# Second halves of weight pairs split by ScalarE and an accumulating transfer in the last half of each MLP, and an eighth seven-product pair in the very last half

## Chip, cores and metric

One core of one Trainium2 chip runs the whole program. The metric is the device time of one launch in microseconds, as the median of several runs.

## What is computed

A two-layer trunk on x of 256 rows and 2048 columns in float32: layer 0 mixes tokens with a convolution module, layer 1 with latent attention, and each is followed by an MLP with squared ReLU. The change lies in the MLPs, in the product with `w2` (8192 x 2048):

```python
D_MODEL, SEQ, D_FF, DEPTH = 2048, 256, 8192, 2

def sq_relu_mlp(h, w1, w2):
    return jnp.square(jax.nn.relu(h @ w1)) @ w2

for layer in range(DEPTH):
    ...
    h = rms_norm(x, norm_mlp_g[layer])
    x = x + sq_relu_mlp(h, mlp_w1[layer], mlp_w2[layer])
return rms_norm(x, final_norm_g)
```

## The kernel before

Every float32 factor is split into a high part `hi` (rounded to the matmul's float32r type) and a low part `lo` = value minus `hi`. A product of two split factors is three matmuls (`mm3`, L203 to L205): high times high, low times high, high times low. ScalarE makes `hi` by a copy (L170, L497), VectorE makes `lo` by a subtraction (L174, L498). Weights come from HBM by SyncE's queue into `raw` (L160). Three `raw` buffers of 8 KB a partition and six buffers each of `hi` and `lo` of 4 KB (WB = 6) rotate, so the split of later weights runs ahead of TensorE by what these hold.

An MLP (`mlp`, called once for each layer) runs in two **halves** of the 8192 inner columns. A half first computes its 4096 inner columns (the up-projection, L655 and L656, from the turned input `xt` that lies at the right end of SBUF), eight groups of 512 columns; each group is squared, scaled and split again (L673 to L687). Then comes the down-projection with 4096 rows of `w2`, in two **passes** of 1024 output columns each (`Sums`, with all 8 PSUM banks). In a pass a unit of work is a **pair** of 128 rows by 1024 columns, for both blocks of 128 tokens:

- A *plain* pair takes 2 x 2 x 2 products of three matmuls, 24 in all. Its two rows are two weight pieces of 1024 columns; each is split by one ScalarE copy and one VectorE subtraction.
- A *mixed* pair takes seven products instead of eight (21 matmuls) in a Strassen-like scheme. VectorE pays for it: `mixed_weights` (L490 to L512) forms sums of weight blocks in place (L505, L506, L507) and splits seven blocks (three subtractions of 1024 columns and one of 512).

`MIXED` names the mixed pairs of each half: eight of sixteen (0, 1, 4, 5, 8, 9, 12, 13) in three halves, and seven, without 13, in the last half of layer 1. In a pass with eight, the order is plain, plain, mixed, mixed, plain, mixed, mixed, plain and so on; the last two are plain. Before the last pair `join` puts the mixed sums u1, u6, u7, u5 into `xs` (L586 to L591), and after it `close` adds the other four (L601, L604). In some passes the additions into `xs` are accumulating transfers from GpSimd's queue (`put`, L578).

The last pass of layer 1 (columns 1024 to 2047) runs through `product_A`: plain units of 4 x 128 rows by 512 columns for column block 2 (24 matmuls each), with mixed pairs (both column blocks) put between them by `between`, and then the plain units of column block 3. Before the change there are five units (the second has 2 x 128 rows and 12 matmuls), with 2, 1, 2 and 2 mixed pairs between them.

Each engine runs its instructions in the order in which the program lists them. That order was fixed when the program was built, and so were the places of the buffers.

```python
    def split_half(raw, h, eng):
        return lower_half(*upper_half(raw, h), eng)
    ...
        def plain(self, w, k, hi, lo, k0, end, middle=None):
            at_j = split(load([rows(w, k, 2, self.n * NB, 2 * NB)], 2), nc.vector)
    ...
            units = [list(range(4 * g, 4 * g + 4)) for g in plain]
            units[1:1] = [[2 * p, 2 * p + 1] for p in ps if p // 2 in mixed]
```

Of the kernel before, what the change touches and what calls it, by code (L numbers as in the profile page):

```python
# [38 lines left out]
PAD_RIGHT = 48  # L39
PAD_KV = 8  # L40
PAD_O = 56
WB = 6
# [37 lines left out]
def trunk_kernel(  # L80
# [83 lines left out]
    def upper_half(raw, h):  # L164

        _, nj, cols = raw.shape
        js = slice(h * nj // 2, (h + 1) * nj // 2)
        hi = wpool.tile([P, nj // 2, cols], F32R, tag="hi", name=nm("hi"), bufs=WB)
        lo = wpool.tile([P, nj // 2, cols], F32R, tag="lo", name=nm("lo"), bufs=WB)
        nc.scalar.activation(hi, raw[:, js, :], AF.Copy)  # L170
        return hi, lo, raw[:, js, :]

    def lower_half(hi, lo, raw, eng):
        eng.tensor_tensor(lo, raw, hi.bitcast(F32), op=ALU.subtract)  # L174
# [17 lines left out]
    def load_split(srcs, nj):  # L192
        return split(load(srcs, nj), nc.vector)
# [222 lines left out]

    def product_A(
        w, k_lo, nk, hi, lo, add, prepare, blocks=range(NNB), due=(), finish=None, before=None,
        units=None, banks=None, begun=None, beside=None, room=None,
    ):  # L420

        due = list(due)
# [9 lines left out]
        for n in blocks:  # L432
            ps = [acc_tile() for _ in range(T)] if banks is None else banks[n]

            n_end = 3 if finish is not None and n == blocks[-1] else 0
            wjs = []

            def products(u, t, to_end=True):
                for j, k in enumerate(units[u]):
                    mm3(  # L440
                        ps[t], hi(k, t), lo(k, t), *wjs[u](j),
                        first(ps[t]), u == nu - 1 - (not to_end) and k == units[u][-1],
                    )

            for u, ks in enumerate(units):
                if u == 0 and beside is not None:
                    beside(n, -1, due)
                wjs.append(load_split([rows(w, k_lo + ks[0], len(ks), n * NB, NB)], len(ks)))
                if u < nu - n_end:
                    for j, k in enumerate(ks):  # L450
                        for t in range(T):
                            mm3(ps[t], hi(k, t), lo(k, t), *wjs[u](j), first(ps[t]), u == nu - 1 and k == ks[-1])
                if banks is None:
                    while due:
                        prepare(due.pop(0))
                    step(-(-20 * 4 // nk) + 1 if nk > 4 * NNB else 6)
                elif n == blocks[-1]:
                    for _ in range(len(due) if n_end else min(1, len(due))):
                        prepare(due.pop(0), out=room)
                if beside is not None:  # L460
                    beside(n, u, due)
            if n_end:
                before()
                for t in range(T):


                    halves = t == T - 1
                    for u in range(nu - n_end, nu - halves):
                        products(u, t, not halves)
                    add(n, ps, t)  # L470
                    if not halves:
                        prepare(n, t)
                    else:
                        h = NB // 2
                        for c in range(2):
                            o = acc_tile()[:, :h]
                            for j, k in enumerate(units[-1]):
                                wh, wl = (w[:, c * h : (c + 1) * h] for w in wjs[-1](j))
                                mm3(o, hi(k, t), lo(k, t), wh, wl, j == 0, k == units[-1][-1])
                            add(n, {t: o}, t, c)  # L480
                            prepare(n, t, c)
                    finish(t)
            else:
                for t in range(T):
                    add(n, ps, t)
                due.append(n)
# [25 lines left out]
    def mixed_inputs(v, fh, fl):  # L512
# [15 lines left out]
        nc.vector.tensor_tensor(a12, a12, a11, op=ALU.subtract)  # L528
        halves(a, 3, 4)

    class Sums:


# [25 lines left out]
        def plain(self, w, k, hi, lo, k0, end, middle=None):  # L559

            at_j = split(load([rows(w, k, 2, self.n * NB, 2 * NB)], 2), nc.vector)
            order = [(j, c, t) for j in range(2) for c in range(2) for t in range(T)]
            if end:
                order.sort(key=lambda r: r[1:])
# [40 lines left out]
                        self.put(t, c, o)  # L605

    put_off = []

    def mlp(layer, ssq, next_gain, finish=None, before=None, beside=None, after_up=None):

        with ExitStack() as cx:
# [22 lines left out]
            for hf in range(HALVES):  # L634
# [70 lines left out]
                    sums.mixed(w, k_lo + 4 * g + 2 * b, gs[g][0][:, b], gs[g][1][:, b], i == len(ms) - 1)  # L705

                split_end = last and finish is not None
                for n in range(0, NNB - 2 * split_end, 2):
                    sums = Sums(n, not last or split_end)
                    ks = [2 * p for p in ps]  # L710
                    at, head = 0, HEAD[n // 2]
                    for i, k in enumerate(ks):
                        upto = (len(ms) * (i - head + 1) + (head > 1) * (len(ks) - head - TAIL)) // (len(ks) - head - TAIL + 1)
                        while at < min(upto, len(ms)):
                            mixed_quad(sums, at)
                            at += 1
                        if i == len(ks) - TAIL + 1:
                            sums.join(room)
                        at_end = i == len(ks) - 1
                        sums.plain(  # L720
                            w, k_lo + k, hi, lo, k, at_end,
                            (lambda: [prepare(due.pop(0), out=room, rest=rest) for _ in range(len(due))]) if at_end else None,
                        )
                    sums.close(room)
                    while rest:
# [5 lines left out]
                if split_end:  # L731
# [2 lines left out]
                    units = [list(range(4 * g, 4 * g + 4)) for g in plain]  # L734
                    units[1:1] = [[2 * p, 2 * p + 1] for p in ps if p // 2 in mixed]
                    nu, at_ = len(units), [0]

                    def between(n, u, due):
                        if n == n2 and u < nu - 1:
                            while at_[0] < min(len(ms), -(-len(ms) * sum(map(len, units[: u + 1])) // sum(map(len, units[:-1])))):  # L740
                                mixed_quad(sums, at_[0])
# [2 lines left out]
                            sums.join(room)  # L744

                    if after_up is not None:
                        after_up()
                    product_A(
                        w, k_lo, nkh, hi, lo, add, prepare, range(n2, NNB), due,
                        finish=(lambda t: finish(nssq, t)) if finish is not None else None,  # L750
                        before=lambda: before(nssq),
                        units=units, banks={n2 + c: [sums.e[t][c] for t in range(T)] for c in range(2)},
                        begun=sums.begun, beside=between, room=room,
                    )
            return nssq

# [1099 lines left out]
    with ExitStack():  # L1856
        gfs = []

        def load_gf():
            gfs.append(right_pool("gf", 1).tile([P, D], F32, name="gf"))  # L1860
# [83 lines left out]
```

## Time and profile before

| | |
|---|---|
| device time, three runs | 1933.95, 1933.99, 1934.88 us; median 1933.99 |
| span of the profiled execution | 1932.5 us, so 1.5 us of the median lie around it |
| layer 0, second half: up-projection, pass 1, pass 2 | 641.26, 818.78, 900.39 to 980.72 us |
| layer 1, second half: up-projection, pass 1, pass 2 | 1582.34, 1759.85, 1842.14 us; last matmul at 1924.45 |

Matmuls overlap: one is listed with 390 ns, but the next starts 0.23 us after it. How long a stage takes is therefore read from starts, or from a stretch's length over its count of matmuls. `PE` is TensorE, `PEld` its weight loads, `DVE` VectorE, `ACT` ScalarE, `POOL` GpSimd and `SP` SyncE.

### The profile page before, as it was taken

What the parts mean: (1) busy time and instruction counts of PE and PEld (TensorE: products, weight loads), DVE (VectorE), ACT (ScalarE), POOL (GpSimd) and SP (SyncE); (2) the same over time, 40 slices, a digit from 0 to 9 for tenths busy, and PEclk for the clock granted to TensorE, in tenths of its full rate; (3) what the DMA queues carried; (4) which work ended last, traced back from release to release, by engine and by line L of the source; (5) the groups of instructions that cost most, each with busy time, mean ns of one, the idle gap of its engine ahead of it and who ended that gap; (6) DMA issues with size and microseconds to landing.
All of it is one profiled execution on the core that took longest, in us unless ns stands there. A gap on an engine that the chain in (4) does not pass through costs nothing.

```text
span 1932.5 us, 28477 instructions
## 1 busy us (share of the span) xinstructions
PE 1921.0 (99%) x10725; PEld 1681.5 (87%) x10725; DVE 1592.2 (82%) x2457; ACT 1095.6 (57%) x1636; POOL 249.0 (13%) x208
## 2 busy tenths in 40 slices
PE   9999999999999999999999999999999999999998
PEld 8999888888888888888898998888888888888887
DVE  7999988877999776799976766877789987678998
ACT  5667755554555545555576655555555554455554
POOL 6999200000010100000001420000000010000000
PEclk9999999999999999999999999999999999999999
DMA  7766456665585866655656545465646776665774
GB/s 230 214 183 189 153 189 206 193 194 177 175 251 194 263 195 187 194 174 196 217 176 175 142 134 192 155 216 186 188 162 225 222 248 212 191 196 175 231 219 150
DMA packets 230427, 375.50 MB, mean 194 GB/s; under 512 B 16392, under 2 KB 107792, under 8 KB 230032
## 3 DMA queue, kind: packets, MB, share of 16 engines
q1 hardware_dynamic: 224640, 363.28, 58.7%
q0 software_dynamic: 4320, 7.87, 2.2%
q10 hardware_dynamic: 1328, 2.52, 0.4%
q8 instruction: 84, 1.38, 0.3%
q14 instruction: 55, 0.45, 0.1%
HBM read 363.68 MB, written 2.10 MB: 189 GB/s over the span
## 4 chain that ended last, share of the span: by engine, by line
PE 97%; DVE 2%; DMA 0%; ACT 0%; issue 0%; ACTq 0%; DVEq 0%
PE acc L655 24%; PE acc L205 15%; PE acc L203 15%; PE acc L204 15%; PE acc L656 13%; PE acc L823 8%; PE acc L1287 2%; DVE sum L910 1%; DMA xs<-in_x 0%; PE acc L1535 0%; PE acc L1566 0%; PE acc L1565 0%; PE acc L1536 0%; PE acc L1564 0%; PE acc L1537 0%; PE tr L267 0%
## 5 line engine op out<-in xcount | busy, mean ns | idle before, releaser
L174 DVE TENSOR_TENSOR lo<-raw,hi 128x1024 fp32r<-128x1024 f32 (+2 forms) x509 | 602.2, 1197 | 232.3 <-ACT hi L170 226.6
L170 ACT ACTIVATE hi<-raw 128x1024 fp32r<-128x1024 f32 (+2 forms) x574 | 583.9, 1036 | 361.1 <-PE acc L655 203.7
L655 PE MATMUL acc<-xt,hi 128*128 128x512 f32 x2048 | 710.6, 390 | 0.0
L656 PE MATMUL acc<-xt,lo 128*128 128x256 f32 x2048 | 577.5, 282 | 0.0
L655 PEld LDWEIGHTS acc<-xt,hi 128*128 128x128 f32 x2048 | 384.3, 188 | 80.7
L656 PEld LDWEIGHTS acc<-xt,lo 128*128 128x128 f32 x2048 | 387.1, 189 | 0.2
L497 ACT ACTIVATE hi<-raw 128x1024 fp32r<-128x1024 f32 x248 | 228.7, 948 | 228.3 <-DVE raw L505 134.0
L498 DVE TENSOR_TENSOR lo<-raw,hi 128x1024 fp32r<-128x1024 f32 x248 | 263.9, 1087 | 27.6 <-ACT hi L497 22.5
L203 PE MATMUL acc<-hi,sh 128*128 128x512 f32 x514 | 200.1, 389 | 0.0
L205 PE MATMUL acc<-lo,sh 128*128 128x512 f32 x514 | 200.1, 389 | 0.0
L203 PE MATMUL acc<-hi,gh 128*128 128x512 f32 (+1 forms) x516 | 200.0, 388 | 0.0
L205 PE MATMUL acc<-lo,gh 128*128 128x512 f32 (+1 forms) x516 | 199.9, 387 | 0.0
L204 PE MATMUL acc<-hi,gl 128*128 128x512 f32 (+1 forms) x516 | 199.9, 387 | 0.0
L823 PE MATMUL acc<-xt,hi 128*128 128x256 f32 x1024 | 180.2, 281 | 0.3 <-ACT b L1106 0.2
L204 PE MATMUL acc<-hi,sl 128*128 128x512 f32 x450 | 175.1, 389 | 0.0
L578 POOL DMA_DIRECT2D xs<-v x30 | 26.5, 994 | 1136.4 <-DVE lo L174 703.2
L910 DVE SCALAR_TENSOR_TENSOR sum<-ub,w_dw,sum 128x256 f32<-128x256 f32 x409 | 164.3, 481 | 3.6 <-ACT sum L880 3.0
L174 POOL TENSOR_TENSOR lo<-raw,hi 128x1024 fp32r<-128x1024 f32 x65 | 155.0, 2410 | 17.3 <-ACT hi L170 17.3
L823 PEld LDWEIGHTS acc<-xt,hi 128*128 128x128 f32 x1024 | 154.8, 188 | 1.1 <-ACT xt L1090 0.6
L823 PE MATMUL acc<-xt,lo 128*128 128x256 f32 x512 | 139.2, 279 | 0.0
L205 PEld LDWEIGHTS acc<-lo,sh 128*128 128x128 f32 x514 | 96.5, 188 | 20.4 <-DVE lo L498 0.3
L204 PEld LDWEIGHTS acc<-hi,gl 128*128 128x128 f32 x516 | 96.9, 188 | 19.9
(314 smaller groups left out, 2531.3 us busy)
## 6 DMA issues: line engine op xcount, KB each, us to landing
raw<-in_mlp_w SPq DMA_DIRECT2D x255, 1024.0 KB, 5.5
raw<-in_conv_w_pw SPq DMA_DIRECT2D x62, 512.0 KB, 5.1
raw<-in_conv_w_pw SPq DMA_DIRECT2D x16, 1024.0 KB, 5.1
raw<-in_mla_w_o SPq DMA_DIRECT2D x16, 1024.0 KB, 5.7
raw<-in_mla_w_kv_up SPq DMA_DIRECT2D x32, 256.0 KB, 3.9
xs<-v POOLq DMA_DIRECT2D x30, 256.0 KB, 7.8
raw<-in_mla_w_in SPq DMA_DIRECT2D x8, 576.0 KB, 3.8
raw<-in_mla_w_in SPq DMA_DIRECT2D x4, 1024.0 KB
```

The lines of the kernel that those rows point to most:

```text
L170: nc.scalar.activation(hi, raw[:, js, :], AF.Copy)
L174: eng.tensor_tensor(lo, raw, hi.bitcast(F32), op=ALU.subtract)
L203: nc.tensor.matmul(ps, sh, mh, start=start, stop=False)
L204: nc.tensor.matmul(ps, sl, mh, start=False, stop=False)
L205: nc.tensor.matmul(ps, sh, ml, start=False, stop=stop)
L497: nc.scalar.activation(hi, src, AF.Copy)
L498: nc.vector.tensor_tensor(lo, src, hi.bitcast(F32), op=ALU.subtract)
L655: nc.tensor.matmul(ps[b], wh[:, bs], xhl(k), start=k == 0, stop=False)
L656: nc.tensor.matmul(ps[b][:, :S], wl[:, bs], xh(k), start=False, stop=k == KC - 1)
L823: nc.tensor.matmul(pss[c][b][:, :S], w[i][:, bs], (xh, xl)[j](k), start=k == i + j == 0, stop=end and k == k0 + nk - 1 and (i, j) == terms ...
L910: nc.vector.scalar_tensor_tensor(out=out, in0=ubs[c][:, w : w + S], scalar=tap(c, w), in1=base, op0=ALU.mult, op1=ALU.add)
L1287: nc.tensor.matmul(ps2[b][t], x_kt(k, t), w[:, bs], start=k == g == i == 0, stop=k == KC - 1 and i == len(group) - 1,)
```

## The change

In the second half of each layer (`last`), the second row of a plain pair is no longer split through `hi`, `lo` and VectorE. `side_parts` loads it into `raw`, ScalarE writes its negative, rounded, to `sidel`, a transfer on GpSimd's queue adds the same weights from HBM to it (so that `sidel` is value minus high part), and ScalarE writes `sideh`. These two have three buffers each, in the place of `xt`, which the second half no longer needs after its up-projection. They are made three units of work ahead (`SIDE_LEAD`): for all plain pairs but the first in pass 1, for those up to the last two in pass 2 of layer 0, and for the second halves of three of the four units in the last pass of layer 1. The first row of such a pair is loaded by itself (512 KB). In layer 0 `xt` is opened again at the last plain pair of pass 2, where the next input is turned. The final gain `gf` takes a place in the new pool.

The last half of layer 1 has eight mixed pairs like the others. Its last pass then has four units with 3, 3 and 2 mixed pairs between them.

```diff
-MIXED = {(layer, half): (0, 1, 4, 5, 8, 9, 12) + (13,) * (layer + half < 2) for layer in range(2) for half in range(2)}
+MIXED = {(layer, half): (0, 1, 4, 5, 8, 9, 12, 13) for layer in range(2) for half in range(2)}
+SIDE_BUFS, SIDE_LEAD = 3, 3
...
+    def side_parts(src, pool):
+        h, l = (pool.tile(list(src.shape), F32R, tag=f"side{c}", name=nm(f"side{c}")) for c in "hl")
+        raw = load([src], src.shape[1])
+        nc.scalar.activation(l, raw, AF.Copy, scale=-1.0)
+        nc.gpsimd.dma_start(l, src, accum_op=ALU.add)
+        nc.scalar.activation(h, raw, AF.Copy)
+        return h, l
...
+            if second is None:
+                at_j = split(load([rows(w, k, 2, self.n * NB, 2 * NB)], 2), nc.vector)
+            else:
+                raw = load([rows(w, k, 1, self.n * NB, 2 * NB)], 1)
+                h, l, _ = upper = upper_all(raw)
+                lower_half(*upper, nc.vector)
+                at_j = lambda j: second if j else (h[:, 0, :], l[:, 0, :])
...
+                    def look(j):
+                        if side is None or j >= len(work) or work[j][0] == "mixed":
+                            return
+                        i = work[j][1]
+                        if i > 0 and (n == 0 or i < len(ks) - TAIL):
+                            seconds[i] = sums.ahead(w, k_lo + ks[i], side)
+                    for j in range(SIDE_LEAD):
+                        look(j)
...
+                    for j, (kind, i) in enumerate(work):
+                        look(j + SIDE_LEAD)
...
+                        if at_end and side is not None and due:
+                            open_xt(f"xt{layer}b")
...
+                        if n == n2:
+                            for v in {-1: (1, 2), 0: (3,)}.get(u, ()):
+                                ks = units[v][2:]
+                                src = rows(w, k_lo + ks[0], 2, n * NB, NB)
+                                seconds[n, v] = side_parts(src, side)
```

Two places in the engines' order carry the prediction. The first is ScalarE at the start of pass 1 in layer 0. `v` rows take the up-projection's last group out of PSUM, `gh` rows split it, `hi_1191` and its followers are the first mixed pair. Before:

```order
L170 ACTIVATE hi_1186_8390<-raw_1185_8388 128x1024
L170 ACTIVATE hi_1188_8394<-raw_1185_8388 128x1024
L497 ACTIVATE hi_1191_8424<-raw_1190_8422 128x1024
L673 ACTIVATE v_1169_8327<-acc_1143_8153 128x256
L673 ACTIVATE v_1169_8327<-acc_1144_8154 128x256
L673 ACTIVATE v_1170_8336<-acc_1145_8155 128x256
L497 ACTIVATE hi_1193_8428<-raw_1190_8422 128x512
L673 ACTIVATE v_1170_8336<-acc_1146_8156 128x256
L686 ACTIVATE gh_1167_8325<-v_1169_8327 128x512
L686 ACTIVATE gh_1167_8325<-v_1170_8336 128x512
```

Of the change, at the same place (`side..1180` and `1181` belong to the second plain pair, `1189` and `1190` to the third, `1214` to the fourth, `hi_1196` begins the first mixed pair):

```order
L179 ACTIVATE hi_1193_8410<-raw_1192_8408 128x1024
L712 ACTIVATE v_1169_8327<-acc_1143_8153 128x256
L712 ACTIVATE v_1169_8327<-acc_1144_8154 128x256
L712 ACTIVATE v_1170_8336<-acc_1145_8155 128x256
L712 ACTIVATE v_1170_8336<-acc_1146_8156 128x256
L550 ACTIVATE sidel_1181_8359<-raw_1182_8360 128x1024
L552 ACTIVATE sideh_1180_8358<-raw_1182_8360 128x1024
L550 ACTIVATE sidel_1190_8402<-raw_1191_8403 128x1024
L725 ACTIVATE gh_1167_8325<-v_1169_8327 128x512
L725 ACTIVATE gh_1167_8325<-v_1170_8336 128x512
L552 ACTIVATE sideh_1189_8401<-raw_1191_8403 128x1024
L512 ACTIVATE hi_1196_8440<-raw_1195_8438 128x1024
```

The copies of the first mixed pair moved from ahead of the group's last evacuation to behind it and behind four new copies.

The second place is the start of the last pass of layer 1. Rows on `acc` are `close` of pass 1, the last of them takes the bank that pass 1's last matmul writes. On ScalarE, before, where `hi_2800` and `hi_2802` begin the first mixed pair of the last pass:

```order
L497 ACTIVATE hi_2800_17769<-raw_2799_17767 128x1024
L497 ACTIVATE hi_2802_17773<-raw_2799_17767 128x512
L604 ACTIVATE v_2784_17713<-acc_2665_17091 128x512
L497 ACTIVATE hi_2804_17780<-raw_2799_17767 128x1024
L604 ACTIVATE v_2785_17716<-acc_2667_17093 128x512
```

Of the change (`hi_2830` and `hi_2832` are the first unit, `side..2834` and `2835` the second half of the last unit, `hi_2838` begins the first mixed pair):

```order
L172 ACTIVATE hi_2830_17838<-raw_2829_17836 128x1024
L172 ACTIVATE hi_2832_17842<-raw_2829_17836 128x1024
L639 ACTIVATE v_2813_17806<-acc_2682_17153 128x512
L552 ACTIVATE sideh_2834_17870<-raw_2836_17872 128x1024
L639 ACTIVATE v_2814_17809<-acc_2684_17155 128x512
L550 ACTIVATE sidel_2835_17871<-raw_2836_17872 128x1024
L512 ACTIVATE hi_2838_17879<-raw_2837_17877 128x1024
L512 ACTIVATE hi_2840_17883<-raw_2837_17877 128x512
```

The first mixed pair's first copies moved from ahead of both copies of `close` to behind them and behind the two side copies.

More of the change, by code (lines that the diff above doesn't have):

```diff
@@ L418, in product_A @@
         w, k_lo, nk, hi, lo, add, prepare, blocks=range(NNB), due=(), finish=None, before=None,
-        units=None, banks=None, begun=None, beside=None, room=None,
+        units=None, banks=None, begun=None, beside=None, room=None, seconds=None,
     ):
@@ L707, in mlp @@
                 split_end = last and finish is not None
+                side = side_pool(f"side{layer}") if last else None
                 for n in range(0, NNB - 2 * split_end, 2):
@@ L711, in mlp @@
                     at, head = 0, HEAD[n // 2]
+                    work = []
                     for i, k in enumerate(ks):
```

43 lines of the change are left out of this document (34 added, 9 removed).

## The prediction

> **What bounds the kernel now.** I read the page's first and fourth part, then busy time by stretches over the passes that the change touches.
>
> ```profile
> PE 1921.0 (99%) x10725; PEld 1681.5 (87%) x10725; DVE 1592.2 (82%) x2457; ACT 1095.6 (57%) x1636; POOL 249.0 (13%) x208
> PE 97%; DVE 2%; DMA 0%; ACT 0%; issue 0%; ACTq 0%; DVEq 0%
> ```
>
> ```profile
> core 0: us, PE busy (x) PEld busy (x) DVE busy (x) ACT busy (x) POOL busy (x), PEclk, DMA share, GB/s
> 818.78:900.39 81.61, 81.61 (x362) 67.57 (x361) 78.90 (x89) 45.14 (x52) 0.10 (x1) 1.00 0.55 188
> 900.39:980.72 80.33, 80.33 (x361) 66.39 (x359) 75.84 (x84) 46.79 (x59) 0.14 (x1) 1.00 0.57 192
> 1759.85:1842.14 82.29, 82.29 (x365) 68.13 (x364) 74.71 (x83) 45.34 (x52) 3.50 (x4) 1.00 0.65 214
> 1842.14:1894.50 52.36, 52.36 (x232) 43.36 (x231) 50.98 (x55) 31.12 (x37) 1.75 (x2) 1.00 0.64 197
> ```
>
> The reader is to see that in all four passes TensorE is busy for the whole stretch at full clock. TensorE waits for nothing; 97% of the chain that ended last is its own. So a relief of VectorE is worth nothing by itself. Time can only fall with fewer matmuls, and every new wait of TensorE is paid in full. A stretch counts also the matmuls that straddle its two edges: pass 1 of layer 0 has 8 x 24 + 8 x 21 = 360 matmuls in 81.61 us, 0.2267 us each. A plain pair is then 5.44 us and a mixed pair 4.76 us.
>
> VectorE has little to spare in the same rows: 78.90 of 81.61, and 50.98 of 52.36 in the last one. What it needs for one mixed pair is read where two follow each other in the last pass of layer 1, from sum (L505) to sum:
>
> ```profile
> 1865.59 1.22 DVE L505 TENSOR_TENSOR raw<-raw 128x1024 f32<-128x1024 f32 x1
> 1866.84 0.69 DVE L506 TENSOR_TENSOR raw<-raw 128x512 f32<-128x512 f32 x1
> 1867.57 0.69 DVE L507 TENSOR_TENSOR raw<-raw 128x512 f32<-128x512 f32 x1
> 1868.18 4.25 DVE L498 TENSOR_TENSOR lo<-raw,hi 128x1024 fp32r<-128x1024 f32 x4
> 1872.35 1.22 DVE L505 TENSOR_TENSOR raw<-raw 128x1024 f32<-128x1024 f32 x1
> ```
>
> That is 6.76 us for a pair which TensorE finishes in 4.76 us. The plain work between mixed pairs gives it back.
>
> **The change part by part.** *Matmuls.* The eighth mixed pair takes 21 matmuls in place of 24 in each of two passes: 6 x 0.2267 = **-1.36 us**. All are on the path. This is the whole gain.
>
> *VectorE's subtractions.* 22 pieces leave VectorE, 1.17 us each (two take 2.35 us in the row of 1893.17 below). On the path they are worth nothing, by the stretches above.
>
> *The first transfer of each half.* In pass 1 the second plain pair has no units ahead of it that could cover its transfer. Its negative copy stands on ScalarE behind the last evacuation of the up-projection:
>
> ```profile
> 817.94 1.08 ACT L673 ACTIVATE v<-acc 128x256 f32<-128x256 f32 x3 [0.74 <-PE acc L656]
> 819.45 0.37 ACT L673 ACTIVATE v<-acc 128x256 f32<-128x256 f32 x1
> 1860.32 1.99 ACT L170 ACTIVATE hi<-raw 128x1024 fp32r<-128x1024 f32 x2
> ```
>
> Four evacuations back to back end at about 819.4 and a copy takes 1.0 us, so GpSimd issues the transfer at 820.4. TensorE, which began the pass at 818.78, needs its result in the third matmul of that row, after 24 + 12 + 2 matmuls: 818.78 + 38 x 0.2267 = 827.4. The trace has no accumulating transfer of 512 KB, but it has 30 of 256 KB:
>
> ```profile
> xs<-v POOLq DMA_DIRECT2D x30, 256.0 KB, 7.8
> L578 POOL DMA_DIRECT2D xs<-v x30: 852/883/1342, 547.1 to 1845.4; - x30
> DMA to landing us min/median/max: 3.5/7.8/10.8
> q0 software_dynamic: 4320, 7.87, 2.2%
> ```
>
> They hold 2.2% of 16 engines for 1932.5 us, 1.4 us of all engines each; twice the bytes add 1.4 us. The transfer then lands after 4.9, 9.2 or 12.2 us (least, median, most), at 825.3, 829.6 or 832.6. TensorE waits 0, 2.2 or 5.2 us; I take the median's **2.2 us**. The same order stands at the start of layer 1's second half, so **+4.4 us**, ends 0 and 10.4.
>
> The Trainium skill, page DMA: Bandwidth & Descriptors, section on the anatomy of one DMA on the SWDGE path, puts such a transfer at 2.0 us and bytes over 436 GB/s, an estimate of 3.2 us for 512 KB: by it the result is there at 823.6, nothing is waited for, and my sum would be 4.4 us less. By the same rule 256 KB take 2.6 us where this trace has 7.8 in the median and 3.5 at the least, so the trace does not agree and its rows are used.
>
> *Loads in pass 1.* Three `raw` buffers serve everything. A mixed pair holds one for its load, a copy and VectorE's 6.76 us.
>
> ```profile
> raw<-in_mlp_w SPq DMA_DIRECT2D x255, 1024.0 KB, 5.5
> raw<-in_mla_w_in SPq DMA_DIRECT2D x8, 576.0 KB, 3.8
> ```
>
> That is 5.5 + 1.0 + 6.8 = 13.3 us, and 8.8 for a plain pair (5.5, a copy, 2.3 of subtractions): 22.1 of 3 x 10.2 us that one of each takes on TensorE, 72%. With the change a plain pair takes two buffers, 3.8 + 1.0 + 1.2 for the first row and 3.8 + 2.0 for the second: 25.1 of 30.6, 82%. ScalarE also stops at each side copy until its load has landed, with a mixed pair's copies queued behind, for which VectorE and then TensorE wait. Following the listed order with these durations through pass 1 of layer 0, the last `lo` of the fourth and of the seventh mixed pair come late by 1 and 2 us. Before, none does. Between 0 and 5 us a pass I take half of that, 1.5: **+3.0 us** for both layers, ends 0 and 10. Pass 2 of layer 0 has only five such pieces, and VectorE is there done with the first mixed pair 3 us ahead of need: 0, ends 0 and 2.
>
> *The last pass of layer 1.* It is limited by when VectorE begins its mixed pairs. Before (S is the pass's first matmul, 1842.14):
>
> ```profile
> 1836.14 1.58 ACT L497 ACTIVATE hi<-raw 128x1024 fp32r<-128x1024 f32 x2 [3.16 <-DMA raw<-in_mlp_w]
> 1837.24 1.23 DVE L498 TENSOR_TENSOR lo<-raw,hi 128x1024 fp32r<-128x1024 f32 x1 [1.61 <-ACT hi L497]
> 1841.03 0.60 ACT L604 ACTIVATE v<-acc 128x512 f32<-128x512 f32 x1 [3.31 <-issue]
> 1842.48 0.59 ACT L604 ACTIVATE v<-acc 128x512 f32<-128x512 f32 x1
> 1893.17 2.35 DVE L174 TENSOR_TENSOR lo<-raw,hi 128x1024 fp32r<-128x1024 f32 x2
> ```
>
> VectorE begins at S - 4.9 and puts four additions of 0.6 us between. Up to the seventh mixed pair it has 7 x 6.76 + 2 x 2.35 + 1.3 = 53.3 us of splits, so it is done at S + 50.8. A mixed pair needs its last `lo` in its 18th matmul, 3.85 us in; TensorE comes there at S + 3 x 5.44 + 2.72 + 6 x 4.76 + 3.85 = S + 51.4. There are 0.6 us to spare, which agrees with a trace without a wait.
>
> With the change three mixed pairs follow each other twice. Up to the sixth, VectorE has 6 x 6.76 + 1.17 = 41.7 us of splits, and TensorE comes to its last `lo` at S + 2 x 5.44 + 5 x 4.76 + 3.85 = S + 38.5. So VectorE would have to begin at S - 3.2. But the pair's first copies now stand on ScalarE behind the last evacuation of pass 1, which takes the bank of its last matmul, and behind a side pair whose buffer pass 1's last pair still reads. That is S, then a side copy 1.0, the evacuation 0.6, a side copy 1.0 and the copy itself 1.0: VectorE begins at S + 3.6, and TensorE waits **6.8 us**. The ends: were ScalarE no obstacle, VectorE would still come behind `close`'s two additions, the second of which needs half of the last plain pair (S - 2.7 + 0.6), and two subtractions (2.35), at S + 0.2, a wait of 3.4; if the pair's load, issued about S - 3.4, took the longest time of any transfer above, 10.8, it would be 11.6.
>
> *The rest.* `xt` opened anew, the pad and `gf`'s place add a memset and no wait: the last two plain pairs, 10.9 us of TensorE, lie between the last use of a side buffer and the first write to `xt`. Without that cover the first turning copy would wait up to 5.4 us.
>
> *Sum*, on the profiled span: 1932.5 - 1.4 + 4.4 + 3.0 + 6.8 = 1945.3, and with the 1.5 us around the span **1946.8 us**.
>
> **The rivals.** *Not slower.* VectorE, freed of three subtractions in the last pass and seven before it, begins the last pass's mixed pairs at S - 3.2 or sooner, the transfers land in 7 us, and only the matmuls count: 1934.0 - 1.4 = 1932.6. For it: TensorE has no wait at all before, and VectorE loses 1.17 us at every plain pair. Against it: ScalarE's order. It decides at the first `lo` of that pass: S - 3.2.
>
> *The last pass alone.* The transfers and loads are covered (10 to 12 us of lead for all but the first), and only the last pass costs, 3.4 to 5 us: 1936 to 1937.6.
>
> *The load buffers bind.* If 1 MB loads take 7.2 us and 512 KB 5.5, beside the added transfers, the sum above is 15.0 + 7.7 + 7.5 = 30.2 of 30.6 us, and a pass no longer runs at TensorE's pace. A tenth lost in three passes of 82 us is 24 us more: 1971. Against it: the engines of the transfers are busy for 0.55 to 0.65 of these stretches, and 22 transfers add 22 x 2.8 us over 297.
>
> **How the numbers follow.** My forecast 0.76; not slower 0.11; the last pass alone 0.05; load buffers 0.08. The range from the bounds is 1936 (every unknown at its lower end: 1934.0 - 1.4 + 3.4) to 1960, short of all upper ends together (1967), which no one mechanism brings about. It leaves out the first rival and the last, 0.19. A measurement of this kernel tells about 0.2%, 3.9 us, from no change. Beyond that lie my forecast and the last rival, and not quite all of the forecast's low end: slower 0.83. The first two rivals give no change, 0.16. Faster by 3.9 us would need more than the six matmuls; 0.01.
>
> **What would show it.** In the changed profile, TensorE's matmuls L212 to L214 should have gaps: at about 827.4, in the second plain pair of layer 0's second half, ended by a transfer into `sidel`, of some 2 us, and the like 8.6 us into layer 1's pass 1; in the last pass, ended by VectorE's `lo` of the third, sixth and eighth mixed pairs, some 7 us together, with VectorE busy throughout. VectorE's first `lo` of that pass should come 3 to 4 us behind the pass's first matmul. The forecast is wrong if that `lo` comes before it, or if the second plain pair runs through. If gaps lie instead all along the two first passes, ended by ScalarE behind loads, the load buffers were the larger matter.

## The result, and the profile after

The change takes **1993.97 us** in the median of five runs (1992.92 to 1998.20), against 1934.01 before (1933.95 to 1934.88): a ratio of 1.0313, 95% interval 1.0300 to 1.0325. It is 60 us slower, where 12.8 were forecast and 1960 was the upper end of the range. The profiled execution of the change has a span of 1993.3 us, 60.8 more than that of the kernel before.

The first part of the page and the chain that ended last, of the changed kernel:

```profile
PE 1946.1 (98%) x10719; PEld 1685.5 (85%) x10719; DVE 1579.2 (79%) x2449; ACT 1118.6 (56%) x1662; POOL 269.4 (14%) x232
...
PE 85%; DMA 6%; DVE 5%; ACT 3%; issue 1%; ACTq 0%; DVEq 0%; SPq 0%
PE acc L694 23%; PE acc L695 12%; PE acc L214 12%; PE acc L212 12%; PE acc L213 12%; PE acc L892 8%; DMA raw<-in_mlp_w 5%; PE acc L1356 2%; DVE lo L513 2%; ACT hi L512 1%; DVE sum L979 1%; DVE raw L520 1%; ACT sideh L552 1%; DVE raw L521 0%; ACT sidel L550 0%
```

There are six matmuls fewer and VectorE is busy for 13 us less, both as meant. But TensorE's own share of the chain fell from 97% to 85%, and loads of weights into `raw` (5% of the span, some 100 us) stand in it now. Busy time by stretches shows where: both passes of layer 0's second half in one row, then pass 1 and the rest of layer 1's.

```profile
core 0: us, PE busy (x) PEld busy (x) DVE busy (x) ACT busy (x) POOL busy (x), PEclk, DMA share, GB/s
818.65:1013.50 194.85, 176.48 (x727) 138.11 (x725) 147.27 (x165) 105.85 (x126) 10.79 (x15) 0.96 0.68 201
1792.13:1893.71 101.58, 90.67 (x362) 69.56 (x361) 69.28 (x78) 55.00 (x63) 9.84 (x12) 0.95 0.75 219
1893.71:1985.06 91.35, 85.16 (x372) 67.22 (x372) 82.01 (x101) 50.12 (x68) 5.17 (x5) 1.00 0.62 190
```

Before, these stretches took 162.4 (818.78 to 981.18), 82.3 and 82.3 us (1842.14 to the last matmul at 1924.45). So layer 0 lost 32.4 us and layer 1 28.3; all other stages together lost 0.1. The reader is to see that it is lost in all four passes (17.1 and 15.4 us in layer 0, 19.3 and 9.0 in layer 1), that VectorE, the engine the change relieves, is now idle for a quarter of the first row, and that the granted clock is below 1.00 in the first two rows.

Who ended TensorE's waits in layer 0's second half:

```profile
engine line waited for: us in total, times, longest us
PE acc L212 <- ACT hi L512: 12.6, 10, 3.1
PE acc L214 <- DVE lo L513: 5.1, 9, 0.7
PE acc L214 <- DMA sidel<-in_mlp_w: 0.6, 1, 0.6
```

L512 and L513 are the split of the mixed pairs. It is not the side pieces that come late (0.6 us, once), but the mixed pairs among which they were put. What made these late is read here around 870 us, first in the instructions in order of time, then in the chain of waits:

```profile
860.81 0.33 SPq L162 DMA_DIRECT2D raw<-in_mlp_w  x1
865.01 1.06 ACT L550 ACTIVATE sidel<-raw 128x1024 fp32r<-128x1024 f32 x1 [3.07 <-DMA raw<-in_mlp_w]
865.98 1.04 ACT L512 ACTIVATE hi<-raw 128x1024 fp32r<-128x1024 f32 x1
```

```profile
866.92 1.05 ACT sideh L552
867.98 0.02 issue
868.00 8.68 DMA raw<-in_mlp_w
...
876.78 1.06 ACT hi L512
...
882.20 1.23 DVE lo L513
883.43 0.04 issue
883.48 0.50 PE acc L214
```

Read from the top: at 860.81 a load of 512 KB is issued, 0.03 us after a subtraction has freed its `raw` buffer. It lands 4.1 us later. ScalarE has waited 3.1 us for it, and does the copies that stand in its queue; the second side copy among them (L552) frees the next buffer at 867.97. 0.03 us later the 1 MB load of a mixed pair starts, takes 8.68 us, and only then come the copy, VectorE's work and the matmul that has been waiting. Two loads stand in series, each waiting for a buffer. In the whole trace of these passes every load is issued within 0.04 us of the moment when its buffer comes free.

The loads themselves are longer: 1 MB took 5.8 us in the median of these passes before (5.3 to 6.6), and now:

```profile
q1 hardware_dynamic: 8897, 32.07, 47.1%
q0 software_dynamic: 1728, 6.29, 20.0%
...
raw<-in_mlp_w SPq DMA_DIRECT2D x18, 1024.0 KB, 9.8
raw<-in_mlp_w SPq DMA_DIRECT2D x21, 512.0 KB, 4.7
```

(These are the queues and issues between 820 and 1013 us; a median is that of the loads whose landing the profile shows, four of the 18 and 11 of the 21; the three 1 MB loads more that the chain of waits shows took 8.2, 8.5 and 10.1 us.) Twelve accumulating transfers, queue q0, hold all 16 engines of the transfers for 20% of that time, for a fifth of the bytes of q1.

### The profile page after: what moved, and what is told of

It reads as the page before. It is cut to its first block, busy times and chain, and to the rows that moved or that the text cites. A ratio compares the mean times of both kernels' runs of the same rounds, so it can differ in the third digit from the quotient of the medians.

```text
span 1993.3 us, 28557 instructions
## 1 busy us (share of the span) xinstructions
PE 1946.1 (98%) x10719; PEld 1685.5 (85%) x10719; DVE 1579.2 (79%) x2449; ACT 1118.6 (56%) x1662; POOL 269.4 (14%) x232
## 4 chain that ended last, share of the span: by engine, by line
PE 85%; DMA 6%; DVE 5%; ACT 3%; issue 1%; ACTq 0%; DVEq 0%; SPq 0%
PE acc L694 23%; PE acc L695 12%; PE acc L214 12%; PE acc L212 12%; PE acc L213 12%; PE acc L892 8%; DMA raw<-in_mlp_w 5%; PE acc L1356 2%; DVE lo L513 2%; ACT hi L512 1%; DVE sum L979 1%; DVE raw L520 1%; ACT sideh L552 1%; DVE raw L521 0%; ACT sidel L550 0%
## 5 line engine op out<-in xcount | busy, mean ns | idle before, releaser
L183 DVE TENSOR_TENSOR lo<-raw,hi 128x1024 fp32r<-128x1024 f32 (+2 forms) x481 | 571.5, 1200 | 234.8 <-ACT hi L172 222.6
L172 ACT ACTIVATE hi<-raw 128x1024 fp32r<-128x1024 f32 (+1 forms) x524 | 534.7, 1037 | 346.3 <-PE acc L694 198.7
L512 ACT ACTIVATE hi<-raw 128x1024 fp32r<-128x1024 f32 (+1 forms) x256 | 234.5, 946 | 235.6 <-DVE raw L520 124.9
L513 DVE TENSOR_TENSOR lo<-raw,hi 128x1024 fp32r<-128x1024 f32 (+1 forms) x256 | 271.5, 1088 | 86.4 <-ACT hi L512 82.3
L212 PE MATMUL acc<-hi,sh 128*128 128x512 f32 x512 | 207.2, 405 | 23.0 <-ACT hi L512 23.0
L212 PE MATMUL acc<-hi,gh 128*128 128x512 f32 (+1 forms) x428 | 166.1, 388 | 0.9 <-ACT hi L172 0.9
L214 PE MATMUL acc<-lo,gh 128*128 128x512 f32 (+1 forms) x428 | 165.8, 387 | 0.5 <-DVE lo L183 0.5
L213 PE MATMUL acc<-hi,gl 128*128 128x512 f32 (+1 forms) x428 | 165.9, 388 | 0.0
L183 POOL TENSOR_TENSOR lo<-raw,hi 128x1024 fp32r<-128x1024 f32 x65 | 155.1, 2414 | 17.3 <-ACT hi L172 17.3
L212 PEld LDWEIGHTS acc<-hi,sh 128*128 128x128 f32 x512 | 98.3, 192 | 54.4 <-ACT hi L512 35.5
```

The lines of the kernel that those rows point to most:

```text
L212: nc.tensor.matmul(ps, sh, mh, start=start, stop=False)
L213: nc.tensor.matmul(ps, sl, mh, start=False, stop=False)
L214: nc.tensor.matmul(ps, sh, ml, start=False, stop=stop)
L512: nc.scalar.activation(hi, src, AF.Copy)
L513: nc.vector.tensor_tensor(lo, src, hi.bitcast(F32), op=ALU.subtract)
```

## The experiments

"Layer 0" below is the time from the first matmul of its second half to the first of layer 1's up-projection: 422.5 us before, 455.0 with the change, so that +32.4 is to be explained; "layer 1" is that from the first matmul of its second half to the last: 164.6 and 192.9, +28.3. Three theories were put against each other. **Load buffers:** three loads a round of plain, side and mixed pair share three `raw` buffers and wait for each other. **Transfers:** the accumulating transfers slow every load. **ScalarE's order:** the side copies stop ScalarE ahead of the mixed pairs' copies.

**The two parts apart.** The kernel before with the eighth pair alone:

```
-MIXED = {(layer, half): (0, 1, 4, 5, 8, 9, 12) + (13,) * (layer + half < 2) for layer in range(2) for half in range(2)}
+MIXED = {(layer, half): (0, 1, 4, 5, 8, 9, 12, 13) for layer in range(2) for half in range(2)}
```

> The eighth mixed pair in the last half of layer 1, no side pieces. If the 60 us come with the side pieces, as all theories below say, this stays within 4 us of 1934.0. What it tells apart is my step on the last pass: six matmuls fewer give 1932.6; if VectorE, which has to be done with the sixth mixed pair 12.9 us of TensorE earlier than before with the same work ahead of it, is late without the side pieces too, 1934 to 1938, with waits of L214 on lo in the last pass of layer 1 only.

Measured: 1937.93 us, ratio 1.0018 (1.0009 to 1.0027). Layer 0 is unchanged, layer 1 is 3.1 us longer, all in its last pass. TensorE's waits there:

```profile
PE acc L203 <- ACT hi L497: 1.6, 4, 0.7
PE acc L205 <- DVE lo L498: 0.9, 2, 0.5
```

With the slow start behind each of these waits (the next matmul starts 0.34 us later in place of 0.23) the matmuls' intervals give 4.2 us, against 1.4 us for six matmuls. ScalarE's copies there wait in turn for VectorE's sums (L505, 18.0 us in seven waits), and VectorE itself stands still only once, for 1.8 us. So the eighth pair by itself makes the kernel slower: VectorE cannot finish eight mixed pairs by the time TensorE wants them.

The side pieces alone (the first line above turned round in the changed kernel, and units of two rows passed over):

> Side pieces as in the change (one fewer, in the last pass, where a unit has two rows only), seven mixed pairs in the last half of layer 1. Load buffers, or transfers, or ScalarE's order as the cause: 1985 to 1995, the second half of layer 0 as long as in the change (194.9 us from its first to its last matmul). Had the eighth pair been the larger matter in layer 1: 1960 to 1970.

Measured: 1999.53 us, ratio 1.0333 (1.0319 to 1.0347); layer 0 +31.5, layer 1 +33.2 (in the expectation the second half of layer 0 is its two passes, 194.9 us). The 60 us come with the side pieces. It is more than the 1985 to 1995 expected: in layer 1 they cost more without the eighth pair than with it, for a reason that stays open.

**Buffers of their own.**

```
-SIDE_BUFS, SIDE_LEAD = 3, 3
+SIDE_BUFS, SIDE_LEAD, SIDE_RAW = 3, 3, 2
...
-        raw = load([src], src.shape[1])
+        raw = pool.tile(list(src.shape), F32, tag="sideraw", name=nm("sideraw"), bufs=SIDE_RAW)
+        nc.sync.dma_start(raw, src)
...
-        return right_pool(name, SIDE_BUFS)
+        return right_pool(name, SIDE_BUFS if name == "side0" else 2)
```

> In layer 0 the side pieces are loaded into two buffers of their own and no longer into the three raw buffers; transfers, copies and their order stay. Theory of the load buffers (three loads of a round of plain, side and mixed pair go through three buffers, each is issued only when its buffer is free, so that the round lasts as long as one buffer is held): the second half of layer 0 falls from 194.9 to 163 to 170 us. Theory of the transfers (twelve accumulating transfers slow every load) or of ScalarE's order (the side copies stop ScalarE ahead of a mixed pair's copies): it stays at 185 to 195 us. Layer 1 has only two buffers for the finished side pieces here, which may hold ScalarE up, and is not to be read.

Measured: 1950.03 us, ratio 1.0081 (1.0067 to 1.0094). Layer 0 is 6.8 us longer than before in place of 32.4, its two passes take 169.0 us. (Layer 1, with only two buffers for the finished pieces, +9.8.) Busy time and TensorE's waits in them:

```profile
818.88:987.91 169.03, 164.32 (x724) 135.75 (x723) 143.00 (x161) 105.46 (x124) 10.77 (x15) 0.98 0.77 227
```

```profile
engine line waited for: us in total, times, longest us
PE acc L214 <- DMA sidel<-in_mlp_w: 4.7, 1, 4.7
```

The same twelve transfers run, more densely than in the change (DMA share 0.77 for 0.68), and not one mixed pair is late. This speaks against the transfers as a cause by themselves. It does not decide about ScalarE's order: when this program was built, its copies got other places too. At the start of pass 1 the first mixed pair's four copies stand ahead of the side copies, and from then on the two kinds follow each other differently than in the change. So the run shows what shared buffers and that order cost together.

The one wait left is that for the first transfer, and it is largely this run's own: the piece's load goes to a place that `xt` held, starts at 819.08, and the transfer follows at 824.75, where the change issues it at 820.59.

**No transfers.** The products then use the negated rounded weight alone as lower part.

```
-        nc.gpsimd.dma_start(l, src, accum_op=ALU.add)
```

> The 22 accumulating transfers are left out, so that the lower part of a side piece is only the negated rounded weight; loads, copies and buffers stay. Theory of the transfers: the waits go, 1936 to 1945. Load buffers: the loads get somewhat shorter, but the rotation stays: 1965 to 1985. ScalarE's order: unchanged but for what a side piece itself was late, 1980 to 1992.

Measured: 1962.37 us, ratio 1.0145 (1.0131 to 1.0159); layer 0 +12.1, layer 1 +14.4. The waits in layer 0's second half:

```profile
PE acc L212 <- ACT hi L512: 4.9, 10, 1.0
PE acc L214 <- DVE lo L513: 2.4, 4, 0.7
```

They are those of the change, shorter: the mixed pairs' split, fourteen times. A 1 MB load is back at 5.9 us in the median (four of 18). The time lies below what the load buffers or ScalarE's order alone were expected to leave, and above what the transfers alone were. ScalarE's copies stand in the order of the change here, one for one. So 20.3 of the 32.4 us in layer 0 need the transfers, and 12.1 are what three loads a round in three buffers and ScalarE's order cost with undisturbed loads. With loads in buffers of their own the transfers cost next to nothing, as the next run shows.

What ScalarE's order has in it is read from the trace of the change. The wait of TensorE that ended at 835.39 (2.8 us) is of this kind:

```profile
828.77 0.69 DVE L522 TENSOR_TENSOR raw<-raw 128x512 f32<-128x512 f32 x1
833.34 1.06 ACT L550 ACTIVATE sidel<-raw 128x1024 fp32r<-128x1024 f32 x1 [7.81 <-DMA raw<-in_mlp_w]
834.30 1.04 ACT L512 ACTIVATE hi<-raw 128x1024 fp32r<-128x1024 f32 x1
```

VectorE has finished the sums that this `hi` needs by 829.46, but a side copy stands in front of it and waits 7.8 us for its load. With the wait behind it and the one that ended at 889.97, this kind makes 5.1 of the 18.3 us that TensorE waits in layer 0's second half. Some 10 us go back to five 1 MB loads (issued at 868.00, 889.00, 911.14, 936.71 and 960.62); the first four were issued when a `sideh` copy had freed their buffer. The two causes hang together, since ScalarE's order also sets when `sideh` frees a buffer; no run here takes them apart.

**Buffers of their own, and no first piece.** Layer 1 as before; in layer 0 the buffers of the run above, and the first piece of pass 1 left out:

```
-                        if i > 0 and (n == 0 or i < len(ks) - TAIL):
+                        if i > (n == 0) and (n == 0 or i < len(ks) - TAIL):
...
-                side = side_pool(f"side{layer}") if last else None
+                side = side_pool(f"side{layer}") if last and layer == 0 else None
```

> Layer 1 as before the change. In layer 0 the side pieces have two load buffers of their own, and the first of pass 1, whose transfer nothing covers, is left to VectorE: 11 pieces. If load buffers and that first transfer are the whole price in layer 0: 1934 to 1936, without a wait of TensorE in the second half. If other side pieces are late too once the first is gone: up to 1941, the 6.8 us that the second half of layer 0 was longer with own buffers.

Measured: 1936.26 us, ratio 1.0011 (1.0002 to 1.0020); layer 0 +1.3, just above the first expectation, and TensorE has no wait in the second half. So with buffers of their own the first piece costs 5.5 of the 6.8 us in layer 0, and the other eleven, with their transfers, nothing that a wait shows. The 1.3 us that are left lie in the matmuls' intervals, which are 228.6 ns in the mean in place of 226.8. What this is was not looked into.

**Fewer pieces in the shared buffers.** Layer 1 as before; side pieces only for even `i`:

```
+                        if i > 0 and i % 2 == 0 and (n == 0 or i < len(ks) - TAIL):
```

> Layer 1 as before the change. In layer 0 side pieces only for plain pairs 2, 4 and 6 of pass 1 and 2 and 4 of pass 2, 5 in place of 12, loaded through the three raw buffers as in the change. If every piece costs its share of the 32.4 us of layer 0: 13.5, 1947 to 1948. If the cost sets in where three loads a round fill the three buffers, and two and a half leave room: 1934 to 1940.

Measured: 1936.57 us, ratio 1.0012 (1.0003 to 1.0021); layer 0 +2.4. Five of twelve pieces cost 2.4 of 32.4 us: the price is not one per piece. A price that sets in when every round has three loads fits this, but transfers and side copies fell with the loads, so this run alone does not show it.

**Transfers alone.** Layer 1 as before; in layer 0 twelve accumulating transfers into tiles that nothing reads, without side loads and copies. The first form of it:

```
-                            seconds[i] = sums.ahead(w, k_lo + ks[i], side)
+                            l = side.tile([P, 1, 2 * NB], F32, tag="sidel", name=nm("sidel"))
+                            nc.gpsimd.memset(l, 0.0)
+                            nc.scalar.activation(l[:, 0, :8], ident[:, :8], AF.Copy)
+                            nc.gpsimd.dma_start(l, rows(w, k_lo + ks[i] + 1, 1, n * NB, 2 * NB), accum_op=ALU.add)
```

> The kernel before, with the 12 accumulating transfers of layer 0 added at the places of the change into tiles that nothing reads: no side copies, no side loads, two loads a round in the three raw buffers. Theory of the transfers by themselves: they slow every load and cost most of what leaving them out of the change gave back in layer 0 (20 us): 1950 to 1955. Theory that they cost by lengthening loads of which a rotation of three buffers has no time left: with two loads a round each load has some 7 to 9 us from its issue to its copy, and little is lost, 1934 to 1940.

Measured: 1952.72 us, ratio 1.0096 (1.0082 to 1.0110). It is not to be read as meant: ScalarE waited 27.9 us for the clearing of tiles, and the transfers, for which nothing else had to be ready, started in bursts, all twelve between 820.4 and 867.2. The second form clears three tiles once, ahead:

> The run with transfers alone once more, without what spoilt it: there ScalarE waited 27.9 us for the clearing of tiles, which waited for earlier transfers. Here three tiles are cleared once, ahead, and ScalarE only marks each (8 columns) at the place of the side copies of the change, so that the 12 transfers of layer 0 start at such intervals; side loads and copies are absent, two loads a round go through the raw buffers. Transfers that cost by themselves: 1945 or more. Transfers that cost only where no time is left in the load buffers: 1934 to 1937.

Measured: 1949.96 us, ratio 1.0079 (1.0064 to 1.0095), layer 0 +15.6; but again not at the change's spacing. The twelve were issued between 820.7 and 859.1, where the change spreads them over 140 us. What it shows is a bound, transfers back to back (queues from 820 to 870 us):

```profile
q0 software_dynamic: 1728, 6.29, 67.6%
q1 hardware_dynamic: 1156, 4.44, 25.0%
```

The loads issued meanwhile at 832.6, 846.0 and 848.2 took 12.2, 10.1 and 13.8 us, and all but about one of the 15.6 us were lost before 867; from then on the kernel ran as before. That the transfers lengthen loads is shown by this and by the run without them; that they cost little at the change's spacing, where two loads a round go through the shared buffers, rests on the run with buffers of their own and no first piece. By its expectation this run would speak for transfers that cost by themselves; back to back they do.

**GpSimd in place of side pieces.** The eighth pair in the kernel before, and in the last pass:

```
-                wjs.append(load_split([rows(w, k_lo + ks[0], len(ks), n * NB, NB)], len(ks)))
+                eng = nc.gpsimd if beside is not None and n == blocks[0] and u < 3 else nc.vector
+                wjs.append(split(load([rows(w, k_lo + ks[0], len(ks), n * NB, NB)], len(ks)), eng))
```

> The eighth mixed pair without side pieces, and the subtractions of the first three plain units of the last pass of layer 1 on GpSimd, which does nothing there, in place of VectorE. If VectorE's sum of work up to the sixth and the eighth mixed pair is what the eighth pair's waits come from (4.2 us in all): 7 us less of it take them away, and only the six matmuls are left, 1932.6 to 1933.6, ratio 0.9993. If GpSimd's slower subtractions (2.4 us for 1.2) hold a load buffer or VectorE itself up: 1936 to 1942.

Measured: 1944.28 us, ratio 1.0052 (1.0039 to 1.0064). VectorE's and GpSimd's subtractions in that pass, one row of each (mean ns behind the busy time):

```profile
L499 DVE TENSOR_TENSOR lo<-raw,hi 128x512 fp32r<-128x512 f32 x8 | 9.9, 1232 | 0.0
```

```profile
L174 POOL TENSOR_TENSOR lo<-raw,hi 128x1024 fp32r<-128x1024 f32 x5 | 15.0, 3020 | 34.9 <-PE acc L205 18.9 <-PE acc L204 16.0
```

VectorE's 128x512 subtraction took 685 ns with the eighth pair alone and takes 1232 in the mean here: two of the eight ran beside GpSimd and took 2.87 us each, the other six 0.68. Three of 128x1024 beside it took 1.7 to 3.6 us in place of 1.22. VectorE so loses 7.8 us, more than the 7.3 that six subtractions of 1.22 would have taken from it. GpSimd's takes 3020 ns for 2414 in the changed kernel's page. The waits are 10.9 us, and the time lies above both expectations. The Trainium skill, page GPSIMD Engine Reference, section Key points, says that the two share their SBUF interfaces and contend where an instruction of VectorE has two SBUF inputs, as this one has; the trace agrees.

**The last pass with buffers of their own.** First in the kernel before with the eighth pair, side pieces for two units of the last pass only, two buffers of each kind:

> The eighth mixed pair, and side pieces only for the second and third plain units of the last pass of layer 1, loaded into two buffers of their own, with two buffers for the finished pieces. Two subtractions of 1.2 us leave VectorE, of the 4.2 us that the eighth pair alone waits; were nothing else late: 1.8 to 2.4 us of waits against 1.4 us of matmuls, 1934.5 to 1935.5, no better than the kernel before. If the added copies and transfers hold the mixed pairs up as in the change: 1937 to 1942.

Measured: 1937.95 us, ratio 1.0020 (1.0011 to 1.0029), no better than the eighth pair alone. The last pass waits 3.6 us for 4.2; pass 1, where nothing was changed but the space, got 1.4 us of waits, whose cause stays open.

Then the whole change, with buffers of their own in both layers and without the first piece of each; the final norm's gain gives the room (the output is multiplied by another factor):

```
-            gfs.append(pool.tile([P, D], F32, name="gf", bufs=1))
-            nc.scalar.dma_start(gfs[0], final_norm_g.rearrange("(a n) -> a n", a=1).partition_broadcast(P))
+            gfs.append(xs[:, 0, :])
```

> The change with two load buffers of their own for the side pieces of both layers (and three buffers for the finished pieces), the first side piece of each pass 1 left to VectorE, and eight mixed pairs. The room comes from the final norm's gain, whose 8 KB are not loaded: the last multiplication takes the first row of the sums in its place, the same amount of work with another factor. What is left is the last pass of layer 1. My step on it, 6.8 us of waits against 1.4 of matmuls: layer 1's second half 170 us in place of 164.6, 1939 to 1941 in all. If ScalarE's order does not delay VectorE there, and only VectorE's sum of work counts (4.2 us of waits with the eighth pair alone, less 2.3 to 3.5 that the side pieces take from it): 164.0 to 166.0, 1934 to 1936.5 in all.

Measured: 1945.46 us, ratio 1.0052 (1.0036 to 1.0069). Layer 0 +1.2, layer 1 173.9 us, +9.3 (1.5 us more lie ahead of the first MLP). About 7.9 us of waits lie in the last pass, near the 6.8 of the step and outside both expectations of the stage's length. The waits of TensorE in layer 1's second half, and VectorE's work around the start of the last pass, 1846.3:

```profile
PE acc L214 <- DVE lo L513: 4.1, 6, 1.3
PE acc L212 <- ACT hi L512: 1.9, 3, 0.7
```

```profile
1843.32 1.23 DVE L513 TENSOR_TENSOR lo<-raw,hi 128x1024 fp32r<-128x1024 f32 x1 [1.99 <-ACT hi L512]
...
1851.79 0.69 DVE L637 TENSOR_TENSOR xs<-acc,xs 128x512 f32<-128x512 f32 x1 [3.12 <-DMA xs<-v]
...
1857.59 1.23 DVE L513 TENSOR_TENSOR lo<-raw,hi 128x1024 fp32r<-128x1024 f32 x1 [2.10 <-ACT hi L512]
```

VectorE begins the mixed pairs 3 us ahead of the pass here, and then stands still in front of an addition of `close` that waits for a transfer of `put` on GpSimd's queue: that transfer was issued at 1844.4 and landed at 1851.7, and until 1848.7 a side piece's, issued at 1834.9, was under way beside it. VectorE then waits 2.1 us for the next pair's copy, which stands on ScalarE behind an evacuation and two side copies.

## Why the prediction was wrong, step by step

- **What bounds the kernel:** right. Eleven subtractions taken from VectorE without any wait (buffers of their own, no first piece) gained nothing.
- **Matmuls, -1.4 us:** right, six fewer.
- **The first transfer of each half, +2.2 each:** TensorE waited 0.6 us for it in layer 0 and 1.9 in layer 1, within the bounds; the mechanism was right. The transfers took 7.4 and 8.7 us, where 9.2 was forecast. With buffers of their own, where the transfer starts 4.2 us later, TensorE waits 4.7 us in layer 0, and the half clock behind that wait, of which I had not thought, adds 1.8.
- **Loads, +3.0 in the two first passes and 0 in pass 2 of layer 0:** this is the step that failed, by its size. The two passes of layer 0 lost 17.1 and 15.4 us, and pass 1 of layer 1 lost 19.3. The rival "the load buffers bind" had named the condition (three buffers, sum of holding times over 30.6 us) and said where the gaps would lie. In layer 0 25.6 of the 32.4 us go when the side loads leave the shared buffers (and ScalarE's order changes with them). Two things were wrong in the working. First, it took the load times of the profile before, 5.5 and 3.8 us; with the change 1 MB takes 9.8 and 512 KB 4.7, and the same sum, 9.8 + 1.0 + 6.8 for the mixed pair, 4.7 + 1.0 + 1.2 and 4.7 + 2.0 for the plain one, is 31.2 of 30.6 (an estimate: with 8.7, the median when the three loads that the chain shows are counted in, it is 30.1). I had added the transfers' cost to the transfers only, not to the loads beside them. Second, a share of holding time is the wrong test. Without the transfers the sum is 5.9 + 7.8 and twice a load of 4.4 with 2.2 and 2.0, 26.7 of 30.6 or 87%, and 12.1 us are lost all the same, because, as around 870 us, each load waits for the one buffer that comes free next, and ScalarE takes its copies in order, so that one late load passes its delay to the next. The rival's price, 24 us, was still only about half of what own buffers give back, 25.6 us in layer 0 and 18.5 in layer 1.
- **The last pass, +6.8:** VectorE's late start is right, and the waits are within the bounds. The pass begins at 1893.71 and VectorE's first `lo` was forecast 3.6 us behind it. It comes 5.4 us behind, at 1899.11, after the copies that the step names: a side copy, the evacuation, a side copy, the mixed pair's copy. But the first of these waited for its load, 9.8 us by the chain of waits.

```profile
1892.60 2.00 ACT L172 ACTIVATE hi<-raw 128x1024 fp32r<-128x1024 f32 x2 [2.95 <-DMA raw<-in_mlp_w]
1894.51 0.58 ACT L639 ACTIVATE v<-acc 128x512 f32<-128x512 f32 x1
1895.58 1.06 ACT L552 ACTIVATE sideh<-raw 128x1024 fp32r<-128x1024 f32 x1 [0.49 <-DMA raw<-in_mlp_w]
1896.55 0.58 ACT L639 ACTIVATE v<-acc 128x512 f32<-128x512 f32 x1
1897.03 1.05 ACT L550 ACTIVATE sidel<-raw 128x1024 fp32r<-128x1024 f32 x1
1898.02 1.58 ACT L512 ACTIVATE hi<-raw 128x1024 fp32r<-128x1024 f32 x2
```

  The matmuls' intervals give 9.4 us of waits in this pass, 1.9 of them in its first plain unit, whose load came late (L172), and 7.5 at the mixed pairs. The signs were not all as forecast: ScalarE's `hi`, itself behind VectorE's sums, ends most of the waits (5.0 us in eight, 0.7 for a `lo` of a mixed pair), and VectorE is idle for 4.9 of the first 51.3 us. With the load buffers out of the way 7.9 are left; there VectorE waits for a transfer first (3.1 us) and then for ScalarE's order (2.1). And 4.2 come without any side piece.
- **The rest, `xt` and `gf`:** no wait is seen there.
- **Not in the prediction: the clock.** Of the 60.8 us, 11.0 are matmuls at half speed behind waits (55 of them, 0.20 us more each; below).

What stays open: how much of 9.8 us for a 1 MB load is the transfers' share of the engines and how much that loads, freed together, start together; and how much of the 12.1 us without transfers is the buffers and how much ScalarE's order. In the run with own buffers, the same transfers at a higher density left 1 MB loads at 6.7 (four of 17).

## What to carry to other kernels

Before an edit adds loads to a shared set of buffers, count the loads per round against the buffers: where each load is issued the moment a buffer comes free, the buffers are the queue, and a piece that is off VectorE's list still takes its turn in it. A transfer is priced with what it does to the loads beside it, not only by when it lands itself. And relief for an engine that TensorE does not wait for is worth nothing, while everything that the relief needs (a load, two copies, a transfer) can become what TensorE waits for.

## What the runs showed of the hardware

**Half clock after waits that add up.** Three windows of 3.41 us in the changed kernel, each with the one behind it:

```profile
833.52:836.93 3.41, 1.02 (x3) 0.58 (x4) 1.56 (x2) 3.41 (x4) 0.86 (x1) 1.00 0.27 19
836.93:840.34 3.41, 3.41 (x9) 2.69 (x9) 3.41 (x4) 1.77 (x3) 0.00 (x0) 0.50 0.94 225
1854.11:1857.52 3.41, 1.71 (x7) 1.09 (x7) 3.03 (x4) 2.74 (x3) 0.00 (x0) 1.00 0.93 174
1857.52:1860.93 3.41, 3.41 (x10) 2.61 (x9) 3.41 (x4) 0.80 (x2) 0.00 (x0) 0.50 0.92 270
1823.39:1826.80 3.41, 1.95 (x8) 0.97 (x6) 3.06 (x4) 3.41 (x5) 0.86 (x1) 1.00 0.44 49
1826.80:1830.21 3.41, 3.18 (x14) 2.64 (x15) 3.41 (x5) 1.33 (x2) 0.00 (x0) 1.00 0.91 225
```

The first number behind the length is TensorE's busy time, the column behind the five engines the clock. Behind the first two windows the clock is halved, and the matmuls start 0.43 us apart in place of 0.23; behind the third it is not. Seven such stretches lie in the four passes, six of 3.41 us and one of 6.83, and they begin whole multiples of 3.413 us from each other. In every window at full clock that came before one TensorE was busy for 1.71 us or less; no window with 1.95 or more came before one, here or in the five other runs that have such stretches. So the waits of one window count together: in the second of the three they are 1.0 and 0.7 us. The Trainium skill, page TensorE: Matmul & The Clock Gate, section What's actually happening, has the clock fall after at least one idle window of about 3.4 us; the length agrees, but a window in which TensorE was busy for half of it was enough here, so the measurement decides. The 55 matmuls at half clock lost 11.0 us, 1.4 for each 3.41 us.

**Accumulating transfers.** 6.29 MB of them held the 16 engines for 20.0% of 193 us, 6.1 us for each MB; plain loads, 32.07 MB in 47.1%, took 2.8.
